# A decoder trunk with top-2-of-8 experts: narrow expert steps from the second step on, first expert's weights requested ahead of the ranking

## The chip, the cores and the metric

The kernel runs on one core of one Trainium2 chip. The metric is device time in microseconds (us), from start to end of one execution; before the change the median of three runs is 1333.34 us (1332.28 to 1335.16). The engines are named as in the profile: PE multiplies matrices (PEld loads its stationary operand), DVE and ACT work elementwise, POOL does a little of the same, and SP only issues transfers from memory (DMA), strictly in the order of its program: a transfer that must wait holds all that stand behind it.

## The reference

Two decoder layers over 256 tokens of width 1024, all in float32. What matters here is the last part, the experts of the second layer:

```
logits = t @ w_router                       # 256 tokens x 8 experts
top_v, top_i = top_k(logits, 2); w = softmax(top_v)
for e in range(8):                          # D_FF_EXPERT = 3584
    g, u = split(t @ w_gate_up[e]); y = (silu(g) * u) @ w_down[e]
    out += gate[:, e] * y
```

Each expert has 1024 x 7168 + 3584 x 1024 weights, 44 MB; eight experts have 352 MB. The kernel computes an expert only for the tokens that chose it, but it must read all weights. Before the experts come a first layer (recurrent and gated mixers, a dense feed-forward) and the attention mixer of the second layer; the last of these is the output projection, after which the router works. The final norm ends the kernel.

## The kernel before, in words

**Steps.** An expert is cut into seven steps of 512 hidden columns (NJ = 7). A step reads six blocks of 1 MB: four of gate and up, two of down; a block is two loads of 512 KB. So a step is 12 loads, the 56 steps are 672 loads. `gate_up(n)` multiplies the four blocks of step n, and in its middle `between(n)` transposes the activations of step n-1 and runs the small jobs planned for step n; then `down(n-1)` multiplies the two down blocks of the step before.

**Wide and narrow.** The experts are ranked by their token counts. Places 0, 1 and 2 of `PLACES` below WIDE = 3 are wide: 128 token slots, weights split by ACT and DVE into a high and a low part (`whi` and a `raw` tile), three multiplications for one. Expert 0 is always the first wide one, so its weights can be requested before the ranking. The other five are narrow: 64 slots, weights used as they come (`whole`), less work on PE. All others' addresses come from `rt.order`, which ranks the experts on PE and DVE (tiles `count` to `ids`); SP reads the number with `values_load` (TENSOR_LOAD of `ids`, and `full` for the check at the end).

**Order of the steps.** The list `steps` mixes the 21 wide and 35 narrow steps. Before, the first three steps (ALONE) are expert 0's alone; the narrow ones are spread evenly from there, and three are kept for the end (LAST). The ranking is a job planned in the middle of step 0, `one_hot` of the first narrow expert in step 1, and its `gather` (its tokens brought together by PE, tile `yTl`) in step 2.

**Buffers.** All loads go into slots of 512 KB (`raw...`): 14 in the ring and two spares at the start, and 18 more that the attention releases: 34, of which two are always spare. `take` gives the slot at the front of the ring, and puts it at the ring's end again at once (a whole block) or when the half is split. A load waits on SP until the last reader of its slot is done. The outputs of an expert (`gated`, tile `y`) take slots of the same ring, and `scatter` (tokens brought back, `tr<-raw,raw` on PE) frees them; its two halves t = 0 and 1 are planned for steps n+2 and n+3.

**Order on the engines.** From `pinned[0] = True` on, every engine keeps the program's order. `run_ahead` splits up to three blocks ahead of use.

Of the kernel before, what the change touches and what calls it, by code (L numbers as in the profile page):

```python
# [10 lines left out]
F32 = mybir.dt.float32  # L11
# [3 lines left out]
AF = mybir.ActivationFunctionType  # L15
# [13 lines left out]
WIDE = 3  # L29
NARROW = 64  # L30
PLACES = (0, 3, 1, 4, 2, 5, 6, 7)
ALONE = 3
LAST = 3
WINDOW = 4
NEG = -1.0e30
HL_BUFS = 6
# [22 lines left out]
def body(ctx: ExitStack, tc: tile.TileContext, x_in, cst_in, lam_in, sgg_in, sgw_in, eg_in, fg_in, wr_in, fin_in,  # L59
         ew_s, ew_t, ew_o, ff_gu, ff_d, ow_s, ow_t, ow_o, moe_gu, moe_d, out):  # L60
    nc = tc.nc
    pinned = [False]
# [66 lines left out]
    def whole_block(src, k):  # L129

        tiles = []
        for h in range(2):
            r = take([128, 1024], F32)
            queue(r, src[h])
            n = 2048 // k
            tiles += [r[:, i * n:(i + 1) * n] for i in range(k // 2)]
        return tiles

    def split_block(src, k, after=None, loaded=None, cuts=1, log=None):

        tiles = []
        for h, raw in enumerate(loaded or [load(src[h]) for h in range(2)]):
            with behind(*(after[h] if after else ())):
                hi, lo, done = split(raw, cuts)
            n = 2048 // k
            for i in range(k // 2):
                tiles.append((hi[:, i * n:(i + 1) * n], lo[:, i * n:(i + 1) * n]))
        if log is not None:
            log.append(done)
        return tiles  # L150
# [865 lines left out]
    def experts(psum, pool, rt, first=False):  # L1016
# [7 lines left out]
        steps = list(wide)  # L1024
        if slim:

            steps, rest = wide[:ALONE], wide[ALONE:]
            done = 0
            for n, step in enumerate(rest):
                upto = (n + 1) * (len(slim) - LAST) // len(rest)  # L1030
                steps += slim[done:upto] + [step]
                done = upto
            steps += slim[done:]
        at_step = {step: n for n, step in enumerate(steps)}
        ids = {0: 0}
# [1 line left out]
        for s in range(len(steps) + 1):  # L1037
# [6 lines left out]
            if s:  # L1044
                i, j = steps[s - 1]
                blocks += [(i, moe_d, (2 * j + b,), 2, narrow[i]) for b in range(2)]
        ready = []

        def prepare():
            i, weights, at, k, whole = blocks.pop(0)  # L1050
            if i not in ids:
                with tc.issue_after(issued[-1].ins):
                    ids[i] = nc.values_load(rt.ids[0:1, i:i + 1], engines=(SP.engine,), min_val=0, max_val=NE - 1)
            src = weights[(ids[i],) + at]
            ready.append((whole, whole_block(src, k) if whole else split_block(src, k)))

        def run_ahead():
            while blocks and (len(ready) <= LOOKAHEAD or
# [135 lines left out]
        def gate_up(n):  # L1194
            i, j = steps[n]
            xt = X[i]
            if narrow[i]:
                p = psum.tile([128, 512], F32, name="gu")
                for kg in range(2):
                    w = [next_block(), next_block()]  # L1200
                    for k in range(4):
                        for gu in range(2):
                            mm64(p, gu, xt[0][:, 4 * kg + k], w[gu][k], kg == k == 0, kg == 1 and k == 3)
                    if kg == 0:
                        between(n)
                silu(i, j, p)
                times_up(i, j, p)
                return
            ps = []
            for gu in range(2):  # L1210
                p = psum.tile([128, 512], F32, name="gu")
                ps.append(p)
                for kg in range(2):
                    w = next_block()
                    for k in range(4):
                        kk = kg * 4 + k
                        if len(xt) > 2 and j == 0:
                            for c in range(2):
                                mm64(p, c, xt[2][:, kk, 64 * c:64 * c + 64], w[k], kk == 0, kk == 7)
                        else:  # L1220
                            mm3(p, cols(xt, kk, slice(0, 128)), w[k], kk == 0, kk == 7)
                if gu == 0:
                    between(n)
                    if n:
                        silu(i, j, p)
            if n == 0:
                slot_scales(i)
                silu(i, j, ps[0])
            times_up(i, j, ps[1])

        def down(n):
            i, j = steps[n]
            if j == 0:
                Y[i] = [psum.tile([128, 512], F32, name=f"dn{c}") for c in ((2,) if narrow[i] else (0, 1))]
            a = ACTS.pop((i, j))
            last = j == NJ - 1
            for b in range(2):
                w = next_block()
                order = [(k, c) for k in range(2) for c in range(2)]
                if last and b == 1 and not narrow[i]:  # L1240
                    order = [(k, c) for c in range(2) for k in range(2)]
                for k, c in order:
                    start, stop = j == 0 and b == 0 and k == 0, last and b == 1 and k == 1
                    if narrow[i]:
                        mm64(Y[i][0], c, a[0][:, 2 * b + k], w[k][:, NS[c]], start, stop)
                    else:
                        mm3(Y[i][c], cols(a, 2 * b + k, slice(0, 128)), (w[k][0][:, NS[c]], w[k][1][:, NS[c]]),
                            start, stop)
            if last:
                y = gated(i)  # L1250
                f = scatter_narrow if narrow[i] else scatter
                for t in range(2):
                    later(n + 2 + t, lambda t=t: f(i, y, t))

        def gated(i):

# [14 lines left out]
        def later(n, f):  # L1271
            plan.setdefault(n, []).append(f)

        def ranked():
            rt.order(psum)

        for row in rows:
            for i in row:
                if i in follows:
# [7 lines left out]
                    later(at_step[i, 0], lambda i=i: slot_scales(i))  # L1287
                later(at_step[i, NJ - 2], lambda i=i: back(i))
        if first:
            later(0, ranked)  # L1290
            later(1, lambda: one_hot(rows[1][0]))
            later(ALONE - 1, lambda: gather(rows[1][0]))

            small = main.tile([128, 2048], F32, name="yTl")
        else:
            rt.number_slots(CAP, NARROW)
        for _ in range(4 if first else 1):
            prepare()
        one_hot(0, 1 if first else 0)
        last = gather(0, rt.xp if first else ())  # L1300
        if first:
            with behind(last):
                rt.gates()
                run_ahead()
        pinned[0] = True
        for n, (i, j) in enumerate(steps):
            for f in before.pop(n, ()):
                f()
            if first and n == ALONE + 5:
                x_sb = residual()  # L1310
            gate_up(n)
            if first and n == len(steps) - 2:
                fin.extend(take([128, D], F32, keep=True)[0] for _ in range(2))
                issued.append(tc.keep_in_program_order(SP.dma_start(fin[0], fin_in.to_broadcast([128, D]))))
            if n:
                down(n - 1)
# [161 lines left out]
```

## Time and profile before

| | before |
|---|---|
| median of three runs | 1333.34 us |
| the profiled execution: time, span | 1332.39 us, 1330.6 us |
| PE busy | 1273.0 us (96%) |
| DVE, ACT, POOL busy | 683.9, 579.2, 23.0 us |
| read from memory | 422.85 MB, 319 GB/s over the span |
| share of the chain that ended last | PE 38%, DMA 21%, DVE 3%, ACT 1% |

PE counts as busy in nearly the whole span, but its matmuls are pipelined and their ends modelled, so that says little. The expert part runs from 446 us (first expert matmul) to the end; in it the share of the DMA engines and the GB/s of a stretch tell more, beside who held SP up. In rows of one engine the columns are start, length, engine, line, operation, out<-in, and in square brackets idle time before and who ended it.

### The profile page before, as it was taken

What the parts mean: (1) busy time and instruction counts of PE and PEld (TensorE: products, weight loads), DVE (VectorE), ACT (ScalarE), POOL (GpSimd) and SP (SyncE); (2) the same over time, 40 slices, a digit from 0 to 9 for tenths busy, and PEclk for the clock granted to TensorE, in tenths of its full rate; (3) what the DMA queues carried; (4) which work ended last, traced back from release to release, by engine and by line L of the source; (5) the groups of instructions that cost most, each with busy time, mean ns of one, the idle gap of its engine ahead of it and who ended that gap; (6) DMA issues with size and microseconds to landing.
All of it is one profiled execution on the core that took longest, in us unless ns stands there. A gap on an engine that the chain in (4) does not pass through costs nothing.

```text
span 1330.6 us, 18752 instructions
## 1 busy us (share of the span) xinstructions
PE 1273.0 (96%) x6528; PEld 846.1 (64%) x6528; DVE 683.9 (51%) x995; ACT 579.2 (44%) x840; POOL 23.0 (2%) x40
## 2 busy tenths in 40 slices
PE   8999999999999999999999989999889999899985
PEld 7888999998777586445654456355545465455542
DVE  7766666657574675443555253363453553434422
ACT  7775544435563465332453243352342443324321
POOL 1000000000001000000000000000000000000001
PEclk9999999999999989999989998899989999899988
DMA  8455666664637499999979999999999999999994
GB/s 320 143 163 176 187 181 186 185 183 155 208 121 305 156 350 363 408 409 409 409 297 368 410 409 409 409 409 410 409 408 405 405 409 409 407 407 408 403 399 177
DMA packets 117895, 425.23 MB, mean 320 GB/s; under 512 B 13600, under 2 KB 13728, under 8 KB 117792
## 3 DMA queue, kind: packets, MB, share of 16 engines
q1 hardware_dynamic: 117072, 423.30, 83.8%
q8 instruction: 53, 0.87, 0.3%
q10 hardware_dynamic: 720, 0.65, 0.2%
q14 instruction: 50, 0.41, 0.1%
HBM read 422.85 MB, written 1.05 MB: 319 GB/s over the span
## 4 chain that ended last, share of the span: by engine, by line
PE 38%; DMA 21%; DVE 3%; ACT 1%; issue 0%; POOL 0%; SPq 0%; ACTq 0%; DVEq 0%; POOLq 0%
PE gu L74 22%; PE dn L74 13%; DMA raw<-in_moe_gu_dram 12%; DMA raw<-in_moe_d_dram 10%; PE tr L74 4%; DVE raw L74 2%; ACT whi L74 1%; DVE al L74 1%; DVE yTh L74 0%; ACT yTh L74 0%; ACT dn L74 0%; POOL fr L1343 0%; ACT raw L74 0%; SPq L104 0%; ACT ah L74 0%
## 5 line engine op out<-in xcount | busy, mean ns | idle before, releaser
L74 DVE TENSOR_TENSOR raw<-raw,whi 128x1024 fp32r<-128x1024 f32 (+1 forms) x376 | 447.9, 1216 | 270.4 <-ACT whi L74 254.2
L74 ACT ACTIVATE whi<-raw 128x1024 fp32r<-128x1024 f32 (+1 forms) x376 | 386.1, 1052 | 266.1 <-DMA raw<-in_moe_d_dram 116.6
L74 PE MATMUL gu<-raw,yTl 128*64 128x512 f32 x1120 | 269.3, 621 | 0.0
L74 PE MATMUL gu<-whi,yTh 128*128 128x512 f32 x640 | 209.9, 399 | 2.3 <-ACT at L74 2.3
L74 PEld LDWEIGHTS gu<-raw,yTl 128*64 128x64 f32 x1120 | 82.3, 142 | 156.3 <-issue 144.6
L74 PEld LDWEIGHTS gu<-whi,yTh 128*128 128x128 f32 x640 | 121.6, 190 | 39.6 <-ACT whi L74 8.1
L74 PE MATMUL dn<-raw,yTl 128*64 128x512 f32 x560 | 127.1, 596 | 0.5 <-ACT yTl L74 0.5
L74 PE MATMUL gu<-raw,yTh 128*128 128x512 f32 x320 | 126.2, 394 | 0.0
L74 PE MATMUL wk<-hTl,whi 128*128 128x256 f32 x336 | 95.2, 283 | 0.9 <-DVE hTl L74 0.9
L74 PE MATMUL wk<-hTh,whi 128*128 128x256 f32 x336 | 95.3, 284 | 0.1
L74 PE MATMUL wk<-hTh,raw 128*128 128x256 f32 x336 | 95.0, 283 | 0.0
L74 PEld LDWEIGHTS dn<-raw,yTl 128*64 128x64 f32 x560 | 38.5, 137 | 76.1 <-issue 67.0
L74 ACT ACTIVATE yTl<-tr 128x256 f32<-128x256 f32 x35 | 13.4, 382 | 168.8 <-PE tr L74 168.7
L74 PE MATMUL dn<-whi,ah 128*128 128x512 f32 x168 | 70.5, 420 | 12.7 <-ACT ah L74 12.7
L74 PE MATMUL dn<-whi,al 128*128 128x512 f32 x168 | 68.9, 410 | 1.8 <-DVE al L74 1.7
L74 PEld LDWEIGHTS gu<-raw,yTh 128*128 128x128 f32 x320 | 61.0, 191 | 12.0 <-DVE raw L74 0.2
L74 DVE SCALAR_TENSOR_TENSOR at<-gu,gs,at 128x512 f32<-128x512 f32 x21 | 15.8, 750 | 102.3 <-PE gu L74 100.2
L74 PE MATMUL dn<-raw,ah 128*128 128x512 f32 x168 | 68.3, 406 | 0.0
L74 PEld LDWEIGHTS wk<-hTl,whi 128*128 128x128 f32 x336 | 64.4, 192 | 1.6 <-DVE hTl L74 1.1
L74 PEld LDWEIGHTS wk<-hTh,whi 128*128 128x128 f32 x336 | 64.4, 192 | 0.9 <-ACT hTh L74 0.5
L74 PEld LDWEIGHTS wk<-hTh,raw 128*128 128x128 f32 x336 | 64.4, 192 | 0.0
L74 ACT ACTIVATE yTl<-gu,gs 64x512 f32<-64x512 f32 x35 | 23.8, 681 | 76.4 <-PE gu L74 76.0
(323 smaller groups left out, 1612.6 us busy)
## 6 DMA issues: line engine op xcount, KB each, us to landing
raw<-in_moe_gu_dram SPq DMA_DIRECT2D x448, 512.0 KB, 10.1
raw<-in_moe_d_dram SPq DMA_DIRECT2D x224, 512.0 KB, 10.1
raw<-in_ff_gu_dram SPq DMA_DIRECT2D x44, 512.0 KB, 3.7
raw<-in_ff_d_dram SPq DMA_DIRECT2D x22, 512.0 KB, 3.6
raw<-in_ew_t_dram SPq DMA_DIRECT2D x16, 512.0 KB, 4.3
raw<-in_ow_t_dram SPq DMA_DIRECT2D x16, 512.0 KB, 3.7
raw<-in_ew_s_dram SPq DMA_DIRECT2D x8, 512.0 KB, 7.2
raw<-in_ew_o_dram SPq DMA_DIRECT2D x8, 512.0 KB, 3.5
```

The lines of the kernel that those rows point to most:

```text
L74: i = f(*args, **kw)
```

## The change

- The list of steps is made from `GAPS`: so many narrow steps stand ahead of each wide one. Step 0 is expert 0's first, steps 1 and 2 are narrow, then one wide, two narrow, and so on. Three narrow steps stand ahead of the first step of the second and third wide expert. The last three steps stay narrow, and the last five steps are the same as before.
- `load_early`: the first eleven blocks of expert 0 after its first four are requested right behind these (22 loads), ahead of the ranking; `split_block` takes them later.
- The ranking, the `one_hot` of the first narrow expert and a small activation that brings the Silu table in come before step 0; the `gather` of the first narrow expert comes at the end of step 0's `gate_up`.
- Step 0's first product is written to the bank `dn2`.
- Both halves of `scatter` are planned for step n+2.
- The residual copies are made in step 5, not 8.

```diff
-ALONE = 3
-LAST = 3
+GAPS = (0, 2, 2, 1, 2, 1, 2) + (3, 1, 2, 1, 2, 1, 2) + (3, 1, 1, 2, 1, 1, 1)
+EARLY = 11
...
-            steps, rest = wide[:ALONE], wide[ALONE:]
-            done = 0
-            for n, step in enumerate(rest):
-                upto = (n + 1) * (len(slim) - LAST) // len(rest)
-                steps += slim[done:upto] + [step]
-                done = upto
+            steps, done = [], 0
+            for step, gap in zip(wide, GAPS):
+                steps += slim[done:done + gap] + [step]
+                done += gap
             steps += slim[done:]
...
-            ready.append((whole, whole_block(src, k) if whole else split_block(src, k)))
+            ready.append((whole, whole_block(src, k) if whole else
+                          split_block(src, k, loaded=early.pop((i, at), None))))
+
+        def load_early():
+            for i, weights, at, k, whole in [b for b in blocks if b[0] == 0 and not b[4]][:EARLY]:
+                early[i, at] = [load(weights[(0,) + at][h]) for h in range(2)]
...
-                p = psum.tile([128, 512], F32, name="gu")
+                p = psum.tile([128, 512], F32, name="gu" if n or gu else "dn2")
...
                 silu(i, j, ps[0])
+                if first:
+                    gather(rows[1][0])
...
-                    later(n + 2 + t, lambda t=t: f(i, y, t))
+                    later(n + 2, lambda t=t: f(i, y, t))
...
-            later(0, ranked)
-            later(1, lambda: one_hot(rows[1][0]))
-            later(ALONE - 1, lambda: gather(rows[1][0]))
...
+        if first:
+            load_early()
         one_hot(0, 1 if first else 0)
         last = gather(0, rt.xp if first else ())
         if first:
             with behind(last):
                 rt.gates()
-                run_ahead()
+            pinned[0] = True
+            rt.order(psum)
+            one_hot(rows[1][0])
+            run_ahead()
+
+            ACT.activation(pool.tile([128, 1], F32, name="nil"), ones[:, :1], AF.Silu)
         pinned[0] = True
...
-            if first and n == ALONE + 5:
+            if first and n == 5:
                 x_sb = residual()
```

On SP's queue before the change, around the place where it reads the ranking (`in_moe_gu_dram`: gate and up, `in_moe_d_dram`: down; the number behind raw is the slot, in which some names occur twice):

```order
L104 DMA raw10_5106<-in_moe_gu_dram 128x1024
L104 DMA raw11_5176<-in_moe_d_dram 128x1024
L104 DMA raw0_5178<-in_moe_d_dram 128x1024
L104 DMA raw1_5200<-in_moe_d_dram 128x1024
L104 DMA raw15_5202<-in_moe_d_dram 128x1024
L1393 TENSOR_LOAD full_4861
L1393 ISA x2
L1053 TENSOR_LOAD ids_4869
```

and there after it, with the first narrow loads behind:

```order
L105 DMA raw10_4774<-in_moe_gu_dram 128x1024
L105 DMA raw11_4776<-in_moe_gu_dram 128x1024
L1400 TENSOR_LOAD full_4864
L1400 ISA x2
L1052 TENSOR_LOAD ids_4872
L1052 ISA x2
L105 ISA
L105 DMA raw1_4907<-in_moe_gu_dram 128x1024
```

Before, 32 loads of expert 0 stand ahead of the reading; after, 30. The next ten, the slots raw1, raw15, raw14, raw18 to raw23 and raw0, are narrow; the eight in the middle are the slots that step 0's own gate and up leave.

On DVE before the change, between the gates (`gr`) and the ranking (`count`), the splits of the next blocks (`raw<-raw,whi`) stand:

```order
L74 COPY gr<-rl_4786 128x2
L74 TENSOR_TENSOR raw_4805<-raw_4800,whi 128x1024
L74 TENSOR_TENSOR raw_4809<-raw_4802,whi 128x1024
L74 TENSOR_TENSOR raw_4826<-raw_4821,whi 128x1024
L74 TENSOR_TENSOR raw_4830<-raw_4823,whi 128x1024
L74 COPY count<-tr 128x8 x2
```

and after it the ranking begins in front of the last piece of expert 0's tokens (`yTh<-tr`), with the gates between its rows:

```order
L75 SCALAR_TENSOR_TENSOR yTh<-acc,cst,yTh 128x128 x3
L75 COPY count<-tr 128x8 x2
L75 MEMSET count 128x1
L75 TENSOR_TENSOR eq<-count 128x64
L75 SCALAR_TENSOR_TENSOR yTh<-tr,cst,yTh 128x128
L75 TENSOR_TENSOR rl_4830<-rl_4830,selm 128x16
```

The four splits no longer stand ahead of the ranking.

## Rows read from the trace of the kernel before

**Rows 1.** Windows of the expert part: engines' busy us, granted clock, DMA share, GB/s
```profile
440.00:470.00 30.00, 27.16 (x135) 14.82 (x134) 20.23 (x67) 13.62 (x28) 0.70 (x1) 0.90 0.52 190
480.00:520.00 40.00, 40.00 (x192) 29.54 (x191) 27.98 (x29) 22.50 (x24) 0.00 (x0) 0.96 0.88 320
520.00:680.00 160.00, 157.22 (x733) 86.89 (x732) 72.86 (x82) 61.46 (x80) 0.00 (x0) 0.98 1.03 409
680.00:720.00 40.00, 39.89 (x183) 23.57 (x183) 19.16 (x22) 13.33 (x18) 0.00 (x0) 1.00 0.75 284
720.00:1300.00 580.00, 553.75 (x2468) 300.13 (x2466) 244.71 (x255) 209.74 (x252) 0.00 (x0) 0.96 1.03 407
```

**Rows 2.** SP's waits in 430:470, 480:520, 670:712, 720:1300: total us, times, longest
```profile
SPq L1393 <- DVE full L74: 7.7, 1, 7.7
...
SPq L104 <- PE gu L74: 18.5, 12, 5.3
...
SPq L104 <- PE tr L74: 21.2, 2, 11.5
...
SPq L104 <- DMA raw<-in_moe_gu_dram: 213.6, 285, 1.4
```

**Rows 3.** SP's issues in order of time, 366:520, and then 640:722
```profile
370.13 36.16 SPq L104 DMA_DIRECT2D raw<-in_moe_gu_dram  x16
...
437.18 13.24 SPq L104 DMA_DIRECT2D raw<-in_moe_d_dram  x4
460.18 4.58 SPq L104 DMA_DIRECT2D raw<-in_moe_gu_dram  x8
...
485.70 4.41 SPq L104 DMA_DIRECT2D raw<-in_moe_d_dram  x4
495.62 11.05 SPq L104 DMA_DIRECT2D raw<-in_moe_gu_dram  x8
...
678.14 13.55 SPq L104 DMA_DIRECT2D raw<-in_moe_d_dram  x4
691.93 14.18 SPq L104 DMA_DIRECT2D raw<-in_moe_gu_dram  x8
```

**Rows 4.** DVE in order of time, around the ranking
```profile
448.58 0.35 DVE L74 SCALAR_TENSOR_TENSOR yTh<-acc,cst,yTh 128x128 fp32r<-128x128 f32 x1 [0.17 <-ACT yTh L74]
...
455.87 0.24 DVE L74 COPY count<-tr 128x8 f32<-128x8 f32 x2 [0.99 <-PE tr L74]
...
458.74 0.17 DVE L74 CAST ids<-idf 128x8 int32<-128x8 f32 x1
```

**Rows 5.** PE in order of time: the first step, then the first gather's last part
```profile
446.50 8.78 PE L74 MATMUL gu<-raw,raw 128*64 128x512 f32 x32
...
455.76 7.09 PE L74 MATMUL gu<-raw,raw 128*64 128x512 f32 x32
462.78 0.61 PE L74 MATMUL tr<-gr,oh 128*128 128x2 f32 x4
...
490.17 0.28 PE L74 MATMUL tr<-oh,hTh 128*128 128x64 f32 x1
...
493.74 0.47 PE L74 MATMUL gu<-whi,yTh 128*128 128x512 f32 x1
```

**Rows 6.** Windows, PE alone: wide down, narrow gate_up, narrow down, wide gate_up
```profile
542.90:548.68 5.78, 5.78 (x28) 1.00 1.03 411
548.68:556.15 7.47, 7.47 (x39) 1.00 1.03 410
556.15:559.60 3.45, 3.45 (x18) 1.00 1.03 407
559.60:571.40 11.80, 11.80 (x56) 1.00 1.02 408
```

**Rows 7.** PE in order of time: scatter in the first step of the second wide expert
```profile
689.59 2.64 PE L74 MATMUL tr<-raw,raw 64*128 64x512 f32 x8
```

**Rows 8.** One of the windows after 720 with a pause of PE
```profile
790.00:800.00 10.00, 5.48 (x13) 3.39 (x12) 6.25 (x6) 5.18 (x7) 0.00 (x0) 0.74 1.03 411
```

More of the change, by code (lines that the diff above doesn't have):

```diff
@@ L1046, in experts @@
                 blocks += [(i, moe_d, (2 * j + b,), 2, narrow[i]) for b in range(2)]
-        ready = []
+        ready, early = [], {}
         def prepare():
@@ L1272, in later @@
             plan.setdefault(n, []).append(f)
-        def ranked():
-            rt.order(psum)
         for row in rows:
```

## The prediction

> **What bounds the kernel now.** I read the page's GB/s by slices first, then windows of the expert part, then SP's waits and issues, and PE last. The windows [rows 1] show a transfer rate that is flat: 409 GB/s from 520 to 680 and 407 from 720 to 1300, with DMA share 1.03. Three stretches fall out of it: 190 GB/s in 440:470, 320 in 480:520, 284 in 680:720. The kernel must read 672 loads of 512 KB for the experts; at 409 GB/s a load is 0.524 MB / 409 = 1.282 us. In the flat stretches SP waits above all for earlier transfers (213.6 us in 285 waits after 720 [rows 2]): the queue is full, and nothing on an engine can make it faster. So the end of the kernel is set by when the loads are through, and what the change can win is the time in which the transfers stood still. In 409-GB/s time that is 30 x (1 - 190/409) = 16.1 us, 40 x (1 - 320/409) = 8.7 us and 40 x (1 - 284/409) = 12.2 us [rows 1], 37.0 us in all. PE looks busy everywhere, but its own work is not the bound: a wide step is 11.80 + 5.78 = 17.58 us, a narrow one 7.47 + 3.45 = 10.92 us [rows 6], so 21 x 17.58 + 35 x 10.92 = 751 us, against 672 x 1.282 = 862 us of transfers.
>
> Each stand-still has its own cause.
> *First, 440:470.* 32 loads of expert 0 are out when SP comes to the ranking; the last of them waits for a slot until about 450, and then SP waits 7.7 us for `full` [rows 2, 3]. The ranking's first row on DVE is at 455.87, `ids` is written at 458.74 [rows 4], and the next load goes out at 460.18 [rows 3].
> *Second, 480:520.* Three wide steps in a row take 17.58 us each on PE against 12 x 1.282 = 15.4 us of transfers, and the first step comes late, so the slots fill up. At 485.70 to 490 the 56th load goes out, the next at 495.62 (eight rows from 370.13 on, 16+4+8+4+8+4+8+4) [rows 3]; PE has then used the gate and up of three steps but for half, and one down: 8+8+4+4 = 24. 56 - 24 = 32 loads are held, which is 34 slots less two spares: full. SP's waits there are for PE's gate and up, 18.5 us [rows 2].
> *Third, 680:720.* SP waits 21.2 us in two waits for PE `tr` [rows 2], from 678.7 to 690.8 and again to 705.8, inside two rows of issues [rows 3]. `tr` with a slot as reader is `scatter`; the row at 689.59 [rows 7] is eight passes: the second half of a narrow expert's and the first of the wide one's. So the load at SP's head wants a slot that still holds an expert's output, and the loads behind it stand.
>
> **The change part by part.**
> *Steps.* Number and work of the steps stay; their order moves PE's demand. I count loads held = loads out - loads used by PE, with the transfers running from 455.2 (below), 30 loads being in by then. Step 0's multiplications end at 462.78 [rows 5]; the ranking's 0.6 us only moves ahead of them. The gather of the first narrow expert, 3.57 us (490.17 to 493.74 [rows 5]), now stands behind step 0, so the first narrow step begins at about 466.4; I allow 1.7 us for a spell at the lower clock, by which the first half of step 0 was longer than its second, 8.78 against 7.09 [rows 5]. PE then takes narrow gate_up 7.47, wide down 5.78, narrow gate_up 7.47, narrow down 3.45, wide gate_up 11.80 and so on:
>
> | end of | at us | loads out | used | held |
> |---|---|---|---|---|
> | narrow gate_up, step 1 | 475.6 | 45.9 | 16 | 29.9 |
> | down of step 0 | 481.4 | 50.4 | 20 | 30.4 |
> | gate_up, step 2 | 488.8 | 56.2 | 28 | 28.2 |
> | wide gate_up, step 3 | 504.1 | 68.1 | 40 | 28.1 |
> | gate_up, step 4 | 515.0 | 76.6 | 52 | 24.6 |
> | wide gate_up, step 6 | 543.5 | 98.9 | 76 | 22.9 |
>
> It stays under 32, nearest at 481. So the second stand-still goes: -8.7 us. From step 1 to the last step of expert 0 there are 10 narrow and 6 wide steps: PE needs 10 x 10.92 + 6 x 17.58 = 215 us, the transfers 16 x 15.4 = 246 us. PE gains 31 us or 24 loads, so at the change to the second wide expert only some 5 loads are held and not, as before, most of the ring. A load then is asked for shortly ahead of its use, when the output's slot has long been freed; and both halves of `scatter` one step earlier free it sooner still. So the third goes too: -12.2 us. From there on the flat rate is what is late next, to the end. Bounds: as long as PE is late and slots are the limit, either stays by half: -4.4 and -6.1 at worst.
>
> *Early loads.* They look like the heart of the change and I give them nothing of their own: 30 loads go out ahead of the ranking after the change, 32 before, in the same slots as these come free. They only keep expert 0's blocks first in the queue although narrow steps now stand between them. Their price is that 22 slots are taken out of turn: until the splits give them back, the narrow loads go round in ten slots, and the second narrow step's loads wait until PE has used the first one's. By the table these slots come free 0 to 2 us ahead of when the queue wants them, except two near 469, which wait for step 1 to begin: +1.3 us. For such waits up to 481 I take +1 us, with 0 and +5 as ends.
>
> *Ranking.* On DVE it no longer waits for the four splits: it begins behind the seventh piece of expert 0's tokens, 448.9 [rows 4], and the 2.87 us from `count` to `ids` [rows 4] plus some 1 us for five small gate rows between give `ids` at 452.8. SP's first narrow load goes out 1.44 us after it (458.74 to 460.18 [rows 3, 4]), at 454.2, the transfer starting about 1 us later. That is 6 us earlier, but two loads, 2.6 us, that went out before now stand behind the ranking. The slots it needs are step 0's own; these come free by pairs at about 450.9, 455.3, 459.2 and 462.7 (8.78 and 7.09 us over two pairs each [rows 5]), in time for loads 1.28 us apart from 455.2. So the first stand-still shrinks by between 0 and 3.4 us: I take -2.5 us (and have the +1 above apart). On the other side 3 us more, if the ranking is slowed between the gates' rows.
> *The rest.* `dn2` for step 0's first product and the table loaded early take away a pause of PE at 465; PE's time ahead of 466 is counted above and no other time of PE ends anything. The splits that went ahead of step 0 now stand behind the ranking on ACT and DVE; they are hidden behind the 13 us of PE from 462.8 to the first wide down. The residual copies take three slots out three steps earlier, in a stretch with eight or more free. The last five steps are the same: 0, within 3 us either way.
>
> Sum: -2.5 - 8.7 - 12.2 + 1 = -22.4 us; I keep 1.5 us of it back for waits of under a microsecond each that the table is too coarse for (the flat rate fell from 409 to 407 after 720, 2.8 us over 580): -21. The profiled execution took 1332.39 us, 1.8 more than its span, so 1311.4 in its terms; the median of the three runs is 0.95 above it: 1312.
>
> **The rivals.**
> *The third stand-still stays* (1324): the outputs' slots are still wanted before `scatter` is through. For it: the 12 us of gather and scatter at the change of expert are the same. Against: PE comes there with 24 loads less held. 1312 + 12.2.
> *More goes* (1304): the ranking's 3.4 us in full, no wait in the ring, the 2.8 us of the flat stretch, and 2 us at the end: 1312 - 0.9 - 1 - 1.5 - 2.8 - 2 = 1304. For it: all these are seen in the trace; against: they need all luck at once.
> *Nothing comes through* (1333): the transfers are through 21 us earlier but PE, with more pauses, ends when it did. Against: 751 us of PE work in some 865.
> *Slower: the ring's ten slots* (1353). Place: SP's queue from the second narrow step to expert 0's third step. If the narrow loads get no slot while PE is in wide work, the transfers stand through the down of step 0, and the steps 3 and 6: 5.78 + 17.58 + 17.58 = 41 us, against -21: +20. It decides when the held count reaches 32: at 481 the table has 30.4, so 2 us of a late PE begin it, but each such wait ends with the next block that PE uses, which is why I give the full price little chance.
> *Slower: PE cold* (1344). In 790:800 PE is busy 5.48 us of 10 and the granted clock is 0.74 [rows 8]: behind a pause its clock is at the lower of its levels, 1.2 GHz, for a while. After the change PE waits for loads from about 680 on, not from 790. If each of the last 40 steps lost the 2.6 us of that window, PE's 751 us would be 855, where the 642 loads after the first 30 need 823: 32 us on top of the forecast. Against: after 720 the mean clock is 0.96 [rows 1], and PE waited there too. The Trainium skill says in "TensorE: Matmul & The Clock Gate", section "HAM oscillation — how this bites in real kernels", that matmuls that wait for transfers in every round start every round cold; by that rule this rival would come, and the trace after 720 agrees only for single windows.
>
> **How the numbers follow.** Forecast 0.64, more goes 0.12, third stays 0.12, nothing 0.05, ring 0.05, cold 0.02. The likeliest alone lies in 1306 to 1318. For 8 in 10 the range takes in the cases at 1304 and 1324: 1303 to 1324. A measurement of this kernel can tell 0.2%, 2.7 us, from no change: faster 0.64 + 0.12 + 0.12 = 0.88, same 0.05, slower 0.07.
>
> **What would show it.** Right: after about 470 no window of 40 us under 400 GB/s until the end; SP's waits from 480 on for transfers, not PE `gu` or `tr`; `ids` at about 453; PE waiting for loads from about 680. Wrong: waits of SP for PE `gu` between 468 and 545 of over 5 us in sum (the ring), a stretch near 300 GB/s at the change to the second wide expert (outputs' slots), or a flat rate throughout with an end that has not moved (PE).

## The result and the profile after

| | median, us | all runs, us | ratio to before, 95% interval |
|---|---|---|---|
| before | 1332.81 | 1331.61 to 1335.16 | |
| changed kernel | 1315.11 | 1314.21 to 1316.71 | 0.9866 [0.9849, 0.9883] |
| changed kernel, second set (e0) | 1314.10 | 1313.67 to 1315.47 | 0.9852 [0.9833, 0.9872] |

One further execution of the changed kernel, in which PE ran at about half its pace all through (2511 us; 1144 ns for the narrow gate and up matmul that takes 608 in e0), is left out; the rows below are from the profiled execution of the second set (1314.05 us, span 1312.3). Lines of its code stand a little later: L75, L105 and L1400 for L74, L104 and L1393.

The forecast was 1312, so 21 us less than before; 18 to 19 us came. First the windows that answer to [rows 1], with 470:480 added:

```profile
440.00:470.00 30.00, 28.63 (x158) 15.89 (x159) 12.84 (x65) 10.72 (x26) 0.70 (x1) 0.89 0.53 201
470.00:480.00 10.00, 10.00 (x50) 5.22 (x47) 5.84 (x7) 1.28 (x2) 0.00 (x0) 1.00 0.76 256
480.00:520.00 40.00, 40.00 (x184) 21.22 (x183) 18.93 (x20) 15.00 (x18) 0.00 (x0) 1.00 1.03 410
520.00:680.00 160.00, 158.41 (x720) 87.67 (x720) 75.69 (x78) 65.86 (x78) 0.00 (x0) 0.98 1.03 409
680.00:720.00 40.00, 40.00 (x198) 24.13 (x196) 19.65 (x28) 14.63 (x23) 0.00 (x0) 1.00 1.03 409
720.00:1300.00 580.00, 558.88 (x2520) 310.84 (x2516) 262.66 (x273) 225.25 (x267) 0.22 (x1) 0.97 1.01 400
```

The last number is GB/s. 480:520 went from 320 to 410 and 680:720 from 284 to 409: two of the three stand-stills are gone. (The last window is low because the loads now end before 1300; 720:1280 has 406.) What is left lies in 440:480: 30 x (1 - 201/409) + 10 x (1 - 256/409) = 15.3 + 3.7 = 19.0 us of stand-still, against 16.1 before. The balance is +2.9 - 8.8 - 12.2 = -18.1 us, and the span went from 1330.6 to 1312.3, -18.3. The agreement is closer than these numbers can carry: after 720 some 2 to 3 us more are lost than before (720:1280 has 408 GB/s before and 406 after), which the balance leaves out. A more direct sign is when SP sends out its last eight loads, before and after:

```profile
1295.06 9.11 SPq L104 DMA_DIRECT2D raw<-in_moe_d_dram  x8
...
1277.01 9.17 SPq L105 DMA_DIRECT2D raw<-in_moe_d_dram  x8
```

They go out 18.05 us earlier, and from there to the end of the span it is 35.5 us before and 35.3 after.

Three finer windows of the changed kernel show where the 19 us lie:

```profile
440.00:455.00 15.00, 13.63 (x72) 8.37 (x73) 11.05 (x60) 6.25 (x21) 0.70 (x1) 0.77 0.18 65
455.00:465.00 10.00, 10.00 (x50) 3.40 (x47) 0.00 (x0) 0.00 (x0) 0.00 (x0) 1.00 0.89 341
465.00:480.00 15.00, 15.00 (x88) 9.34 (x88) 7.63 (x11) 5.75 (x7) 0.00 (x0) 1.00 0.79 279
```

That is 12.6 us behind the last early load, 1.7 us, and 4.8 us in 465:480, where the kernel before had none:

```profile
465.00:480.00 15.00, 14.28 (x57) 11.60 (x58) 8.66 (x10) 9.19 (x11) 0.00 (x0) 0.89 1.02 410
```

SP's waits answer to [rows 2]. In 430:456 (who, us in total, times, longest):

```profile
SPq L1400 <- DVE full L75: 14.0, 1, 14.0
SPq L105 <- PE acc L75: 13.1, 4, 11.5
```

In 465:480, in 480:520 and in 670:712 (what stood there before was `gu` 18.5 in 480:520 and `tr` 21.2 in 670:712):

```profile
SPq L105 <- PE gu L75: 8.4, 4, 4.9
...
SPq L105 <- DMA raw<-in_moe_gu_dram: 9.1, 12, 2.0
SPq L105 <- PE gu L75: 7.3, 8, 1.5
...
SPq L105 <- DMA raw<-in_moe_gu_dram: 17.1, 22, 1.4
...
SPq L105 <- PE tr L75: 0.3, 1, 0.3
```

The 7.3 us for `gu` in 480:520 are worth a remark: in the same window the rate is 410 GB/s. Eight waits of at most 1.5 us stand beside transfers that are still on their way, and cost nothing. One wait of 4.9 us in 465:480 empties the queue, and there the rate falls.

SP's issues in that place, in order of time, each row from a view of its own window, answer to [rows 3]:

```profile
453.19 1.90 SPq L105 DMA_DIRECT2D raw<-in_moe_gu_dram  x3
...
456.08 5.48 SPq L105 DMA_DIRECT2D raw<-in_moe_gu_dram  x4
...
462.94 2.62 SPq L105 DMA_DIRECT2D raw<-in_moe_gu_dram  x3
...
470.64 3.17 SPq L105 DMA_DIRECT2D raw<-in_moe_gu_dram  x4
```

DVE around the ranking, for [rows 4]:

```profile
448.69 0.23 DVE L75 COPY count<-tr 128x8 f32<-128x8 f32 x2
...
451.98 0.17 DVE L75 CAST ids<-idf 128x8 int32<-128x8 f32 x1
```

PE, for [rows 5]: the ranking's sum, step 0's two products, the gather, and step 1's first half:

```profile
447.28 1.02 PE L75 MATMUL tr<-selm,ones 128*128 128x8 f32 x4 [0.86 <-DVE yTh L75]
448.23 9.52 PE L75 MATMUL dn<-raw,raw 128*64 128x512 f32 x32
457.58 7.03 PE L75 MATMUL gu<-raw,raw 128*64 128x512 f32 x32
...
465.01 0.28 PE L75 MATMUL tr<-oh,hTh 128*128 128x64 f32 x1
...
468.68 3.65 PE L75 MATMUL gu<-raw,yTl 128*64 128x512 f32 x16
```

`ids` is written at 452.2 and the first narrow load goes out at 453.2. By 465.6 3 + 4 + 3 = 10 narrow loads are out, as many as the ring has slots for them. From then to 470.6 nothing goes out: the load at SP's head wants a slot of step 1's, and step 1 begins at 468.68.

### The profile page after: what moved, and what is told of

The parts are those of the page before. It is cut to its first block, busy times and chain, and to the rows that moved or that the text cites. A ratio compares the mean times of both kernels' runs of the same rounds, so it can differ in the third digit from the quotient of the medians.

```text
span 2509.7 us, 18750 instructions
## 1 busy us (share of the span) xinstructions
PE 2488.6 (99%) x6528; PEld 1373.0 (55%) x6528; DVE 690.1 (27%) x995; ACT 587.1 (23%) x841; POOL 22.4 (1%) x40
## 4 chain that ended last, share of the span: by engine, by line
PE 99%; DMA 0%; DVE 0%; ACT 0%; issue 0%; POOL 0%; SPq 0%; POOLq 0%; ACTq 0%
PE gu L75 40%; PE dn L75 21%; PE acc L75 20%; PE wk L75 13%; PE tr L75 5%; DMA raw<-in_x_dram 0%; ACT dn L75 0%; POOL fr L1350 0%; DVE hTl L75 0%; SPq L178 0%; DVE raw L75 0%; DVE al L75 0%; ACT raw L75 0%; POOL fms L1349 0%; SPq L105 0%
## 5 line engine op out<-in xcount | busy, mean ns | idle before, releaser
L75 DVE TENSOR_TENSOR raw<-raw,whi 128x1024 fp32r<-128x1024 f32 (+1 forms) x376 | 447.4, 1217 | 589.3 <-ACT whi L75 589.2
L75 PE MATMUL gu<-raw,yTl 128*64 128x512 f32 x1120 | 536.0, 1144 | 0.0
L75 ACT ACTIVATE whi<-raw 128x1024 fp32r<-128x1024 f32 (+1 forms) x376 | 386.1, 1051 | 542.8 <-PE acc L75 193.4
L75 PE MATMUL gu<-whi,yTh 128*128 128x512 f32 x640 | 372.8, 674 | 0.0
L75 PEld LDWEIGHTS gu<-raw,yTl 128*64 128x64 f32 x1120 | 100.8, 181 | 359.6 <-issue 348.2
L75 PE MATMUL dn<-raw,yTl 128*64 128x512 f32 x560 | 268.2, 1144 | 0.5 <-ACT yTl L75 0.5
L75 PEld LDWEIGHTS gu<-whi,yTh 128*128 128x128 f32 x640 | 190.4, 298 | 123.5 <-issue 113.5
L75 PE MATMUL gu<-raw,yTh 128*128 128x512 f32 x320 | 215.9, 675 | 0.0
L75 PEld LDWEIGHTS dn<-raw,yTl 128*64 128x64 f32 x560 | 49.9, 181 | 189.6 <-issue 177.4
L75 PE MATMUL wk<-hTl,whi 128*128 128x256 f32 x336 | 147.5, 439 | 1.2 <-DVE hTl L75 1.2
L75 PE MATMUL wk<-hTh,whi 128*128 128x256 f32 x336 | 148.0, 440 | 0.0
L75 PE MATMUL wk<-hTh,raw 128*128 128x256 f32 x336 | 147.6, 439 | 0.0
L75 PEld LDWEIGHTS gu<-raw,yTh 128*128 128x128 f32 x320 | 94.4, 295 | 46.3 <-issue 36.5
L75 PEld LDWEIGHTS wk<-hTl,whi 128*128 128x128 f32 x336 | 116.5, 347 | 3.3 <-DVE hTl L75 1.8
L75 PEld LDWEIGHTS wk<-hTh,whi 128*128 128x128 f32 x336 | 116.2, 346 | 1.8 <-issue 1.7
L75 PEld LDWEIGHTS wk<-hTh,raw 128*128 128x128 f32 x336 | 116.7, 347 | 0.0
L75 PE MATMUL dn<-raw,ah 128*128 128x512 f32 x168 | 113.4, 675 | 0.0
L75 PE MATMUL dn<-whi,al 128*128 128x512 f32 x168 | 113.3, 675 | 0.0
L75 PE MATMUL dn<-whi,ah 128*128 128x512 f32 x168 | 113.1, 674 | 0.0
L75 ACT ACTIVATE ah<-tr 128x512 fp32r<-128x512 f32 x21 | 12.5, 597 | 388.7 <-PE tr L75 388.7
L75 DVE SCALAR_TENSOR_TENSOR at<-gu,gs,at 128x512 f32<-128x512 f32 x21 | 15.8, 751 | 286.3 <-PE gu L75 286.3
L75 ACT ACTIVATE yTl<-tr 128x256 f32<-128x256 f32 x35 | 13.5, 384 | 324.6 <-PE tr L75 324.6
```

Source lines behind the costliest of these rows:

```text
L75: i = f(*args, **kw)
```

## The experiments

Two theories on what is left in 440:480. **Theory D**: the dead time ahead of the first narrow load counts, so earlier `ids` or more early loads would shorten the kernel. **Theory S**: the slots are all taken, so what has been read by 480 is set by when PE frees them, above all by when step 1 begins; early loads and an earlier ranking then only move the stand-still about. The first experiments ask what each part of the change is worth. e0 to e3 ran together, e4 to e7, e8 to e10, and e11 alone; the kernel before had medians of 1333.41, 1333.82, 1334.60 and 1334.42 us beside them, so a difference of about 1 us between runs of different sets says little.

**e0: the changed kernel again.** It is the trace shown above.

> The changed kernel once more, for a trace that can be laid beside the one before. Theory (stand-stills): 440:470 keeps most of its loss (190 to about 215 GB/s), 480:520 is at 400 GB/s or more (320 before), and no stretch of 40 us near 690 is under 400 (284 before); SP's waits from 480 on are for transfers. The time measured already, 1315, says that some 3 us of the predicted 21 did not come; they should be in 440:475. Rival (PE): the rate is flat all the way but the last load lands 20 us earlier and PE ends later after it than before.

**e1: no early loads.**

```diff
-EARLY = 11
+EARLY = 0
```

> The changed kernel without the early loads (EARLY = 0); all else as changed. Theory: the early loads bring nothing over the kernel before, but in the new order of steps they are needed: without them only 8 loads of the expert part can go out ahead of the ranking, not 30, the slots stand empty, 22 x 1.28 = 28 us of transfers fall behind the ranking: 1337 to 1343. Rival (the rank is early enough, or the transfers had slack): under 1325.

1337.93 us (1336.31 to 1338.64), ratio 1.0028 [1.0017, 1.0038]: slower than the kernel before, 23.8 us more than e0. SP's wait for `full`, and two windows:

```profile
SPq L1400 <- DVE full L75: 51.7, 1, 51.7
```

```profile
440.00:455.00 15.00, 14.74 (x67) 10.93 (x68) 10.26 (x56) 6.40 (x21) 0.70 (x1) 0.57 0.00 0
...
465.00:480.00 15.00, 15.00 (x76) 8.59 (x74) 6.96 (x10) 5.51 (x6) 0.00 (x0) 0.77 1.03 409
```

22 loads x 1.28 us are 28.2 us. That 23.8 came and not 28.2 is the first hint at theory S: without early loads 465:480 runs at 409 GB/s, so e0's 4.8 us of stand-still there fall away. Without the early loads the new order of steps is slower than the old one.

**e2: the order of the steps as before, all else changed.** The list gives the old order.

```diff
-GAPS = (0, 2, 2, 1, 2, 1, 2) + (3, 1, 2, 1, 2, 1, 2) + (3, 1, 1, 2, 1, 1, 1)
+GAPS = (0, 0, 0, 1, 2, 2, 2, 1, 2, 2, 2, 2, 1, 2, 2, 2, 1, 2, 2, 2, 2)
```

> The changed kernel with the old order of steps (three wide first, narrow ones spread evenly), everything else as changed. Theory: the slots fill up again in 480:520 (about 330 GB/s, SP waiting for PE gate and up) and 5 to 9 us come back: 1320 to 1324; the third stand-still stays away, because both halves of scatter are a step earlier. Rival (the order does it all): third stand-still back too, 1330 or more. Rival (the order does nothing): 1315.

Median 1328.77, ratio 0.9951 [0.9930, 0.9971]; the seven runs stand in two groups, 1320.8 to 1323.7 and 1328.8 to 1330.0. The profiled one is of 1320.84. Its windows:

```profile
480.00:520.00 40.00, 40.00 (x182) 29.07 (x182) 31.74 (x31) 26.32 (x28) 0.00 (x0) 1.00 0.94 346
680.00:720.00 40.00, 40.00 (x185) 23.04 (x185) 18.77 (x22) 15.05 (x20) 0.00 (x0) 1.00 1.03 409
```

The second stand-still is there with the old order (6.2 us), the third is not. So the order of the steps ends the second; and against e0 it is worth 7 to 10 us in the better group, and 15 by the medians. Why there are two groups no trace shows; their mean clocks over the span are 0.969 to 0.971 and 0.964 to 0.965.

**e3: the kernel before, with both halves of scatter in step n+2.**

```diff
-                    later(n + 2 + t, lambda t=t: f(i, y, t))
+                    later(n + 2, lambda t=t: f(i, y, t))
```

> The kernel before with one edit: both halves of scatter planned for step n+2. Theory: the stand-still in 680:720 is a load at SP's head that wants the slot of an expert's output, so it goes or shrinks to a third, and SP's waits for PE tr there fall from 21 to under 8 us: 1321 to 1326, ratio 0.992 to 0.995. Rival (the ring is simply full there, as in 480:520): no change, 1331 to 1334.

1324.89 us (1324.06 to 1327.05), ratio 0.9933 [0.9918, 0.9949]. 680:720 and SP's wait in 670:712:

```profile
680.00:720.00 40.00, 40.00 (x180) 24.65 (x178) 18.72 (x21) 14.34 (x17) 0.00 (x0) 0.98 0.97 376
```

```profile
SPq L104 <- PE tr L74: 2.1, 1, 2.1
```

One half of the write-back goes a step earlier, and 21.2 us of waiting for `tr` [rows 2] become 2.1, 284 GB/s [rows 1] become 376, and 8.5 us by the medians (1333.41 beside it) are won of the 12.2 that stood there. That most of the third stand-still is an expert's output holding a slot of the ring is shown; 40 x (1 - 376/409) = 3.2 us of it stay.

**e4: nine early blocks, not eleven.**

```diff
-EARLY = 11
+EARLY = 9
```

> The changed kernel with nine early blocks (18 loads) instead of eleven (22). Four loads of 1.28 us fall behind the ranking. Theory D (the dead time ahead of the first narrow load is what counts): +5.1 us against the changed kernel, 1319 us. Theory S (what has been read by 475 us is set by when PE frees the slots of step 0 and begins step 1, and the early loads only move the stand-still from ahead of the ranking to behind it): the 4.2 us lost in 465:475 go, so +1 us, 1315 us, with 465:475 above 400 GB/s.

1314.65 us (1314.42 to 1321.06), ratio 0.9870 [0.9850, 0.9889]: three runs at 1314.4 to 1314.7 and two at 1319.5 and 1321.1. By the median and the three shorter runs, four loads fewer out ahead of the ranking cost 0.5 us, not 5.1: theory S. The two longer runs lie at theory D's 1319 and above. The profiled execution is one of them (1319.54); in it the rate in 465:480 is 306, and PE's clock is low once more, when step 1 should begin.

```profile
465.00:480.00 15.00, 15.00 (x76) 8.67 (x74) 6.96 (x10) 5.07 (x6) 0.00 (x0) 0.77 0.83 306
468.00:474.00 6.00, 6.00 (x28) 4.23 (x29) 2.79 (x5) 3.45 (x4) 0.00 (x0) 0.57 0.99 392
```

```profile
471.53 5.69 PE L75 MATMUL gu<-raw,yTl 128*64 128x512 f32 x16
```

A granted clock near 0.5 is the lower of its two levels, 1.2 GHz for 2.4; step 1's first half takes 5.69 us and begins at 471.53, where e0 has 3.65 and 468.68. So the expectation of over 400 GB/s was not met in this execution, which has both the four loads less and a late step 1 and can't tell the theories apart. The three shorter runs have no trace; that they had no such spell is concluded from their mean clock, 0.981 to 0.982 against 0.972.

**e5: the ranking's sum and rows ahead of the pieces of expert 0's tokens.** The sum goes to free columns of the router's bank, so that it need not wait for another; the rows that need the gates stay behind them (`order_rows`).

```diff
+            pinned[0] = True
+            rt.order(psum)
+            pinned[0] = False
-        last = gather(0, rt.xp if first else ())
+        with behind(*([rt.counted] if first else ())):
+            last = gather(0, rt.xp if first else ())
...
-            p = psum.tile([128, 8], F32, name="tr")
+            p = self.cp
...
-            rt.order(psum)
+            rt.order_rows()
```

> The changed kernel with the ranking's matmul and its rows on DVE put ahead of most of the pieces of expert 0's tokens (the sum goes to free columns of the bank acc); ids should be written near 447 instead of 452. Theory D: the first narrow load goes out 5 us earlier and the end comes 2.5 to 5 us earlier, 1309 to 1312 us. Theory S: only two spare slots can be filled ahead of step 0's own, step 1 begins when it did or some 1 us later, so within 1.5 us of the changed kernel's 1314, and the loss only moves to 465:475.

1314.02 us (1312.62 to 1316.29), ratio 0.9853 [0.9840, 0.9867], e0's. `ids` came at 450.1 to 450.3, 1.9 us earlier than e0's and not 5 (PE was at its lower clock from 442 on), and the loss only moved:

```profile
440.00:455.00 15.00, 14.74 (x72) 11.00 (x73) 10.62 (x60) 6.26 (x21) 0.70 (x1) 0.66 0.30 105
455.00:465.00 10.00, 10.00 (x49) 3.27 (x45) 0.00 (x0) 0.00 (x0) 0.00 (x0) 1.00 0.88 296
465.00:480.00 15.00, 15.00 (x81) 8.36 (x81) 7.49 (x11) 5.75 (x7) 0.00 (x0) 0.89 0.72 245
```

11.1 + 2.8 + 6.0 = 19.9 us, where e0 has 12.6 + 1.7 + 4.8 = 19.1. This agrees with theory S; as `ids` came only 1.9 us earlier, and with PE slower in the traced execution, it is a weak test.

**e7: the kernel before, with the ranking ahead of step 0.**

```diff
-            later(0, ranked)
...
             with behind(last):
                 rt.gates()
-                run_ahead()
+            pinned[0] = True
+            rt.order(psum)
+            run_ahead()
```

> The kernel before with only the ranking put ahead of step 0. Theory D: ids some 6 us earlier, the 32 early loads stay, so 3 to 6 us faster than before: 1327 to 1330. Theory S: the ring is full of expert 0's loads until step 0 uses them, so no more than 1.5 us: 1332 to 1334.

1333.24 us (1331.30 to 1337.75), ratio 1.0002 [0.9990, 1.0014]: nothing, though `ids` came at 453.6 and not at 458.7. The stand-still has moved on to where the kernel before had 410 GB/s:

```profile
465.00:480.00 15.00, 12.67 (x56) 9.51 (x51) 5.70 (x8) 7.39 (x9) 0.00 (x0) 0.89 0.81 270
```

Theory S, and the clearer test of the two: in the kernel before, the ranking's move is worth nothing on its own.

**e8 and e9: the gather between step 0 and step 1, twice, and cut short.** In e8 it is called twice; in e9 only one of its four matmuls per piece is done (the low part and the second half of the tokens are left out for the first narrow expert).

```diff
                 if first:
                     gather(rows[1][0])
+                    gather(rows[1][0])
```

```diff
+                if first and i == rows[1][0]:
+                    PE.matmul(p, rt.hh[:, 0, k * 128:(k + 1) * 128], OH[i][:, 0, :p.shape[-1]], start=True, stop=True)
-                for t in range(1 if k < len(begun) else 0, 2):
+                for t in range(1 if k < len(begun) else 0, 0 if first and i == rows[1][0] else 2):
                     rt.gather(k, p, OH[i], t)
```

> The changed kernel with the gather of the first narrow expert done twice in a row between step 0 and step 1 (32 more matmuls of 0.11 us, 3.6 us on PE). Theory S (what has been read by 480 us is set by when PE begins step 1): +3.6 us, 1317 to 1318 us, with the loss in 465:480 grown from 4.8 to over 8 us of stand-still. Rival (PE has some 100 us to spare over the expert part, so a later PE costs nothing): 0, 1314.

> The changed kernel with 8 instead of 32 matmuls in that gather; it leaves out the low part and the second half of the tokens for the first narrow expert. PE begins step 1 2.7 us earlier. Theory S: -2.7 us, 1311 to 1312, with 465:480 about 330 GB/s. Rival: 0.

e8: 1323.11 us (1321.63 to 1329.02), ratio 0.9923 [0.9906, 0.9940]: 9.0 us more than e0, for 3.6 us of matmuls (the profiled execution, 1321.63, 7.6 us more). Its window, the clock in it, and step 1:

```profile
465.00:480.00 15.00, 15.00 (x91) 11.39 (x91) 7.06 (x10) 4.74 (x6) 0.00 (x0) 0.77 0.39 136
469.50:476.50 7.00, 7.00 (x31) 5.37 (x32) 2.66 (x5) 0.30 (x1) 0.00 (x0) 0.53 0.05 19
```

```profile
474.16 2.80 PE L75 MATMUL gu<-raw,yTl 128*64 128x512 f32 x6
```

```profile
SPq L105 <- PE gu L75: 12.9, 2, 11.7
```

SP stands 11.7 us in one wait in 465:480, 136 GB/s. Step 1 begins 5.5 us later than in e0, 3.6 for the second gather and the rest for a spell at the lower clock that begins within it. The rival (PE has time to spare) is out: ahead of 480 it has none.

e9: 1313.23 us (1311.65 to 1315.29), ratio 0.9837 [0.9824, 0.9850]. By the medians 0.9 us less than e0, by the ratios 2.0, with intervals that overlap: between the two expectations, and no proof alone. In this execution all work from 429 on lies some 2.5 us later than in e0 (the router's matmuls stand at 442.14 for 439.68), and yet step 1 begins when it does there. The stretch as a whole, e9's row and then, of e0, the same:

```profile
440.00:530.00 90.00, 89.32 (x428) 48.31 (x428) 41.64 (x97) 32.60 (x54) 0.70 (x1) 0.94 0.85 331
```

```profile
440.00:530.00 90.00, 88.63 (x436) 46.53 (x437) 41.05 (x96) 30.79 (x51) 0.70 (x1) 0.96 0.83 323
```

90 x (1 - 331/409) = 17.2 us lost against 18.9: less, as S has it, but part of that may be the later start.

**e10: dummy matmuls in PE's pauses ahead of step 0.** In e0 the granted clock is 0.50 from 447 to 453, and step 0's first product takes 9.52 us where the second takes 7.03.

```diff
-                    last = self.busy(3)
+                    last = self.busy(5)
...
-                    self.busy(1)
+                    self.busy(4)
...
-                for t in range(1 if k < len(begun) else 0, 2):
+                for t in 3 * (0, 1) if begun and k == 7 else range(1 if k < len(begun) else 0, 2):
```

> The changed kernel with 13 more small matmuls in PE's pauses between 441 and 447 (2 and 3 dummies beside the ranking of the tokens, and the eighth piece of expert 0's tokens summed three times). If PE's clock falls to 0.50 at 445 because of these pauses, the spell of 7 us goes, PE begins step 1 about 3 us earlier, and by theory S the end comes 3 us earlier: 1311. If the spell has another cause, it stays and the time with it, 1314 to 1315 (0 to +1 for the added matmuls).

1321.84 us (1312.59 to 1324.13, one run of six under 1319), ratio 0.9889 [0.9866, 0.9912]: worse than either expectation. The spell got longer, with PE busy in nearly all of it, and step 0 began at 455.47 (2.1 us of that are a later start of the stretch, by the router's matmuls):

```profile
441.00:444.00 3.00, 3.00 (x29) 3.00 (x28) 1.65 (x8) 1.57 (x4) 0.27 (x1) 1.00 0.91 348
...
444.00:460.00 16.00, 15.74 (x66) 12.54 (x66) 7.87 (x44) 5.94 (x19) 0.43 (x1) 0.50 0.02 6
```

So pauses are not needed for the clock to fall: here PE is recorded busy for 3.00 of 3.00 us in 441:444, and from 444 on the clock is at 0.50. What lowers it is not shown. That a later PE costs time is seen once more: 440:530 has 284 GB/s, 90 x (1 - 284/409) = 27.5 us lost, against 18.9 in e0 (323 GB/s).

**e6 and e11: the changed kernel with the halves of scatter one step apart, as before.**

```diff
-                    later(n + 2, lambda t=t: f(i, y, t))
+                    later(n + 2 + t, lambda t=t: f(i, y, t))
```

> The changed kernel with the two halves of scatter one step apart again. If the order of the steps alone ends the third stand-still (PE comes to the change of expert with few loads held), 1314 to 1316 us and over 400 GB/s in 680:720. If the earlier second half is what ends it, SP's wait for PE tr comes back and with it 5 to 12 us: 1319 to 1326.

> The kernel of e6 again, for a profiled execution of its longer group of times (1319 to 1324; e6's profiled one was 1314.7). If the longer times come from scatter, 680:720 is under 380 GB/s there with SP waiting for PE tr. If they come from another spell of PE at half its clock ahead of step 1, as in e4's profiled execution, 680:720 stays at 409 and the loss stands in 465:520, with the granted clock near 0.5 for some us between 465 and 480.

e6: median 1320.13 (1314.71 to 1323.96), ratio 0.9902 [0.9883, 0.9921]; e11: 1319.44 (1315.50 to 1324.78), ratio 0.9892 [0.9867, 0.9917]. In both 680:720 has 409 GB/s and SP waits 0.5 us or less there for `tr`, so with the new order the third stand-still is gone without the scatter's move. But the times spread, and e11's profiled execution (1318.83 us) shows a cause, at a place that neither expectation named: the change from the first narrow expert to the second. First e11's 680:720 and the window in question; then SP's wait in 636:664, its issues, and the two halves of the scatter:

```profile
680.00:720.00 40.00, 40.00 (x198) 23.41 (x196) 22.03 (x28) 18.61 (x27) 0.00 (x0) 1.00 1.03 409
...
640.00:660.00 20.00, 20.00 (x90) 14.34 (x90) 11.28 (x12) 11.70 (x13) 0.00 (x0) 1.00 0.80 302
```

```profile
SPq L105 <- PE tr L75: 9.5, 1, 9.5
```

```profile
640.16 1.65 SPq L105 DMA_DIRECT2D raw<-in_moe_d_dram  x2
652.31 4.77 SPq L105 DMA_DIRECT2D raw<-in_moe_gu_dram  x8
```

```profile
631.09 1.97 PE L75 MATMUL tr<-raw,raw 64*128 64x512 f32 x2 [1.59 <-DVE al L75]
...
650.98 1.30 PE L75 MATMUL tr<-raw,raw 64*128 64x512 f32 x4
```

The half that is planned a step later runs 20 us later, at 650.98, and SP holds a load for its slot until then: 20 x (1 - 302/409) = 5.2 us lost. In e6's profiled execution (1314.71) the wait is 6.7 us and 366 GB/s, 2.1 us lost. The longest runs of the two, up to 1324.78, have no trace. In e0 PE does all the halves by 631, and the window has no loss:

```profile
640.00:660.00 20.00, 20.00 (x93) 12.85 (x93) 11.59 (x11) 9.66 (x12) 0.00 (x0) 1.00 1.03 409
```

## Why the prediction came out as it did

**The bound: right.** The end is set by when the loads are through: the last loads go out 18.05 us earlier, and the span is 18.3 us shorter. The 1.5 us kept back for small waits came too: the rate after 720 fell from 408 to 406 GB/s.

**Second stand-still, -8.7: right.** 480:520 went to 410 GB/s. e2 shows that it is the order that does it: with the old one the window is back at 346. The margin was thin. Counted from SP's issues and PE's matmuls in e0's trace, 50 loads are out at 480 and 18 used: 32 held, where the table had 30.4 at 481. At 490 and 500 some 29 and 31 are held, where it had about 28.

**Third, -12.2: right in size, with either of two causes enough for most of it, and the reason for one of them mis-sized.** The step named both, the order (PE comes with fewer loads held) and the scatter's move. e3 shows that the move alone does most of it in the kernel before, e6 and e11 that the order alone does all of it there. They do not add up: e3's 8.5 us are not on top. PE was to have gained 24 loads by then and hold some 5. Counted as above, the kernel before holds 25 at 680 (198 out, 173 used) and e0 20 at 690 (213 out, 193 used): PE gained some 11 since 470, where 31 were held (its 215 us leave out the 12 us of gather and scatter that the rivals name), and it is recorded busy for all 40.00 us of 680:720, so the sign "PE waiting for loads from about 680" did not come. The direction fits: at 640, where e6 and e11 stand still, 25 and 26 are held. But the order did a second thing that the prediction does not name: before, the first narrow and the first wide expert end one step apart, and the row at 689.59 [rows 7] writes back parts of both; now they end six steps apart. No run separates the two. What the prediction did not see is that without the move the new order has a stand-still of its own, at the change of narrow expert near 645, 2 to 5 us in two traces.

**First stand-still, -2.5, and the ring of ten slots, +1: here the sum was off.** Together they were forecast at -1.5 us and came to about +3. The time of `ids` (452.8 said, 452.2 measured) and of the first narrow load (454.2 said, 453.2 measured) were right, and the stretch up to 465 lost 14.3 us where it had lost 16.1, -1.8. The mis-sized term is the ring: the early blocks leave the narrow loads few slots, the queue's head waits for step 1, and this cost 4.8 us in 465:480, not 1. The mechanism and the place (two loads near 469) were named. The size was wrong mostly for one reason: step 1 was put at 466.4 and began at 468.68, and the narrow loads that wait for it went out a us earlier than forecast. PE took step 0 up at 448.23 and not at 446.5 plus the ranking's 0.6, after a wait of 0.86 us for DVE's `yTh`, and step 0 ended at 464.6, not at 462.8. The spell in step 0's first half, 1.7 us in the kernel before, grew to 2.5 (9.52 against 7.03); the 1.7 us allowed for one more in step 1 were not needed. Between step 0 and the gather stands a small sum (`tr<-gr,oh`, 0.46 us to the gather's first matmul) that the prediction left out. 2.3 us of a late PE and 1 us of earlier loads make 3.3 us more of waiting, of the 3.8 that were missed; e8 shows the price of PE's time at this place directly.

**Early loads, nothing of their own: right, and the reading "in the same slots" is what e1 and the shorter runs of e4 bear out.** 22 loads are worth 23.8 us against having none; by the medians the last four of them are worth 0.5, since fewer of them leave more slots to the narrow loads.

**The ranking's move: the prediction gave it part of 2.5 us; in the kernel before e7 finds nothing.** There `ids` earlier by 5 us moved the time by a ratio of 1.0002: the limit is the slot, not the address. e5 agrees for 1.9 us in the changed kernel. No run leaves the ranking in step 0 with all else changed, so what its move is worth in the new order is not shown.

**The rivals.** The third stand-still did not stay (409 GB/s). "More goes" needed all of the first stand-still's 3.4 us, and the ring ate it. Of the ring of ten slots the place was right; it costs 5 and not 41 us, since each wait ends with the next block that PE uses. PE cold did not come: after 720 the granted clock is 0.97, against 0.96 before [rows 1]. The rule of the Trainium skill that was named for it ("TensorE: Matmul & The Clock Gate", section "HAM oscillation — how this bites in real kernels"), that matmuls that wait for transfers in every round start every round cold, does not describe this stretch: in it PE is recorded busy for 558.88 of 580 us, and only single windows are at a lower clock. The next section of that page of the Trainium skill, "A second HAM failure mode: psum-queue depth-cycling", tells of a kernel in which short idle times between groups of matmuls make the clock swing. e10, which filled such pauses, does not bear that out for the spell ahead of step 0.

**A sign that was badly chosen.** SP's waits for PE `gu` of "over 5 us in sum" were to show the ring at fault. There are 7.3 us in 480:520 at 410 GB/s. Whether a wait costs is not in its sum, but in the rate of the same window.

**Left open.** The two groups of e2's times; why PE's clock falls behind the small matmuls of ranking and gather in one execution for 7 us (e0) and in another for 14 (e4); what `dn2`, the early Silu table and the earlier residual copies are worth, which no run asks; and whether a kernel that begins step 1 earlier, with the whole gather, wins the 2 us that e9 hints at. None of the kernels tried is measurably faster than the changed one.

## What to carry to other kernels

Turn each window's rate into lost time against the flat rate, give every loss its one owner, and the sum forecasts the end within a few us. Where loads go through a ring of slots in a fixed order, ask of each stand-still whether it is the address, the slot or the consumer that is late: an earlier address is worth nothing while the slots are full (e7), and then the consumer's delay is paid in full (e8), though it may have 100 us to spare elsewhere. A slot that a later stage borrows (an output waiting for its write-back) blocks the whole queue behind it, so write it back before the queue comes round.

## What the runs showed of the hardware

- PE's granted clock falls to about 0.5 right behind the many small matmuls of ranking and gather, even where PE is busy in the records: 447 to 453 in the changed kernel, 444 to 460 in e10 (PE busy 15.74 of 16 us), and 469 to 476 in e8. How long a spell lasts seems to differ between executions of one kernel: e4's two groups, 1314.4 to 1314.7 and 1319.5 to 1321.1, and a single run of e10 at 1312.59 beside five at 1320 to 1324, go with the mean clock over the span (0.981 to 0.982 and 0.972; 0.983 and 0.972 to 0.976).
- A flat 409 GB/s held for 160 us on end (520:680) with one core reading, in the kernel before and in the changed one.
